# Rotating a matrix by 90 degrees: the last macro tile kept whole, with its first output stored in two halves

## The chip, the cores and the metric

One core of one Trainium2 chip. The metric is device time in microseconds (us) of a whole execution, lower is better. The profile's own span is some 1.9 us shorter than the device time of the same execution.

## The reference

```python
def setup_inputs():
    return {"x": np.random.randn(8192, 8192).astype(np.float32), "k": 1}

def reference(x, k):
    return np.rot90(x, k)
```

256 MiB are read and 256 MiB written (268.44 MB each way in the profile). There is no arithmetic; the kernel is about moving bytes.

## The kernel before

The matrix is cut into macro tiles of 1024 rows by 4096 columns. Each one is loaded as eight blocks of 128 rows (2 MB each, from the SP queue), VectorE (DVE) copies each block in eight chunks with the columns inside a group of 128 reversed, TensorE (PE) transposes 128 by 128 pieces into PSUM, ScalarE (ACT) copies PSUM to an output buffer and issues the store (2 MB each, eight per macro tile). The last macro tile is divided in two of 512 rows, and the first output of the first half is emitted ahead of the last rows' copies.

```python
R = 1024; RT = R // P
LAST = [4, 4]                    # row blocks of the last two tiles
W = 4096; CH = 512; F = 4096; FP = 2048

def macro_tiles(N, M):
    tiles = [(r0, RT, c0) for r0 in range(0, N, R) for c0 in range(0, M, W)]
    r0, _, c0 = tiles.pop()
    for n in LAST:
        tiles.append((r0, n, c0))
        r0 += n * P
    return tiles

# pools: a (row blocks) 2 buffers, ar (chunks) 63, o (outputs) 3, PSUM 2
# ... load(): per row block one DMA, then 8 DVE copies ar <- a (cut)

def store(r0, rt, c0, chunks, end):
    rows = rt * P
    PW = 1                       # column groups of one PSUM tile
    while 2 * PW * rows <= FP: PW *= 2
    G = PW                       # column groups of one output
    while 2 * G * rows <= F: G *= 2
    for i, g0 in enumerate(range(0, W // P, G)):
        if end and i % 2 == 0:   # at the end the row buffers serve outputs too
            ot = a_pool.tile([P, F], dt, tag="a")
        else:
            ot = o_pool.tile([P, F], dt, tag="o")
        # ... (cut)
        S = PW if lead or (end and r0 + rows == N and g0 + G == W // P) else G
        if i == 0 and (rt == RT or r0 + rows < N):
            # first output: transposes by row block, as the rows come
            for h in range(G // PW): psum_tile(h)
            for t in range(rt): transposes(t, range(G))
        for h in range(0, G, PW):
            # ... other outputs: transposes here (cut)
            nc.scalar.copy(o[:, G - PW - h : G - h, :], ps[h // PW])
            done = h + PW
            if done % S == 0:
                # ... dst: (g m) f -> m g f (cut)
                nc.scalar.dma_start(out=dst, in_=o[:, G - done : G - done + S, :])
        yield
```

With 1024 rows PW is 2 and G is 4, so an output has 4 groups of 1024 elements and each piece that is contiguous in DRAM is 4 KB. With 512 rows PW is 4, G is 8, and the piece is 2 KB. An output has 2 MB in both cases.

## Time and profile before

| | |
|---|---|
| device time, median of the first 3 runs | 1267.27 us (1266.35 to 1267.58) |
| span of the profiled execution | 1266.1 us |
| PE, DVE, ACT busy | 57%, 28%, 37% |
| mean transfer rate | 425 GB/s |

No compute engine is near full, and the transfers are at their rate from the second slice of the span to the 38th.

### The profile page before, as it was taken

Reading aid. Unit: us, or ns where it says so; the run is one execution under the profiler, and the core shown is the slowest. Engines: PE = TensorE matmul, PEld = TensorE weight load, DVE = VectorE, ACT = ScalarE, POOL = GpSimd, SP = SyncE. Lnnn points to the kernel's source line nnn. Section 1 sums busy time; section 2 is a strip of 40 time slices with the busy share of each in tenths; the row PEclk is TensorE's granted clock in tenths of the full one; section 3 lists DMA queues with packets and bytes.
Section 4 is the critical chain, followed back from the end, with each engine's and each line's share of the span. In section 5 each row is a group of like instructions: output and inputs, shape, how many; then the busy total and the mean of one; then the engine's idle time right before and its main releaser. Section 6 shows DMA issues by size and latency. Waiting matters only on the chain.

```text
span 1266.1 us, 10392 instructions
## 1 busy us (share of the span) xinstructions
PE 718.2 (57%) x4096; PEld 678.6 (54%) x4096; DVE 355.4 (28%) x1024; ACT 466.7 (37%) x257; POOL 0.7 (0%) x6
## 2 busy tenths in 40 slices
PE   1554565556656665556555665555655656556673
PEld 1543455555555555456554655555655655556562
DVE  4423223222232223222232223322232222322210
ACT  0432433433333333343334333343333433343363
POOL 0000000000000000000000000000000000000000
PEclk9977877777776777867778678677686686776797
DMA  9999999999999999999999999999999999999997
GB/s 399 426 428 430 428 429 427 430 429 429 429 429 429 430 428 427 430 429 430 428 430 428 429 429 428 430 428 428 430 430 428 429 429 428 428 428 428 427 399 328
DMA packets 37345, 537.55 MB, mean 425 GB/s; under 512 B 4144, under 2 KB 4144, under 8 KB 4144
## 3 DMA queue, kind: packets, MB, share of 16 engines
q10 hardware_dynamic: 18864, 268.44, 50.0%
q1 hardware_dynamic: 18432, 268.44, 49.7%
q8 instruction: 32, 0.52, 0.2%
q14 instruction: 17, 0.14, 0.0%
HBM read 268.44 MB, written 268.44 MB: 424 GB/s over the span
## 4 chain that ended last, share of the span: by engine, by line
DMA 82%; ACT 14%; PE 1%; issue 1%; ACTq 1%; DVE 0%; SPq 0%
DMA out_dram<-ot 79%; ACT ot L169 14%; DMA a<-in_x_dram 3%; PE pt L148 1%; ACTq L177 0%; DVE ar L108 0%; ACTq L169 0%; SPq L102 0%
## 5 line engine op out<-in xcount | busy, mean ns | idle before, releaser
L148 PE MATMUL pt<-ident,ar 128*128 128x128 f32 x4096 | 718.2, 356 | 528.0 <-ACT ot L169 487.6
L148 PEld LDWEIGHTS pt<-ident,ar 128*128 128x128 f32 x4096 | 678.6, 191 | 567.4 <-ACT ot L169 521.4
L169 ACT COPY ot<-pt 128x2048 f32<-128x2048 f32 x256 | 465.4, 1869 | 756.7 <-DMA out_dram<-ot 727.0
L108 DVE COPY ar<-a 128x512 f32<-128x512 f32 x1024 | 355.4, 421 | 861.1 <-DMA a<-in_x_dram 524.0
L169 ACT ACT_TABLE_LOAD x1 | 1.3, 1283 | 25.5 <-DVE ar L108 25.5
masks.py:199 POOL TENSOR_SCALAR_AFFINE_SELECT ident<-ident 128x128 f32<-128x128 f32 x1 | 0.3, 292 | 0.1
masks.py:197 POOL MEMSET ident<- 128x128 f32 x1 | 0.2, 204 | 0.3 <-POOLq L217 0.3
L217 POOL MEMSET const-bfloat16-1.0<- 128x1 bf16 x1 | 0.1, 102 | 0.0
L217 POOL MEMSET const-uint8-127<- 128x1 uint8 x1 | 0.1, 102 | 0.0
L217 POOL MEMSET const-float32-0.0<- 128x1 f32 x1 | 0.1, 99 | 0.2 <-issue 0.2
L217 POOL MEMSET const-float32-1.0<- 128x1 f32 x1 | 0.1, 99 | 0.0
## 6 DMA issues: line engine op xcount, KB each, us to landing
a<-in_x_dram SPq DMA_DIRECT2D x128, 2048.0 KB, 16.8
out_dram<-ot ACTq DMA_DIRECT2D x125, 2048.0 KB, 25.5
out_dram<-ot ACTq DMA_DIRECT2D x6, 1024.0 KB, 27.3
```

Source lines behind the costliest of these rows:

```text
L108: nc.vector.tensor_copy(out=ar[:], in_=a[:, j * CH : (j + 1) * CH].rearrange("r (b m) -> r b m", m=P)[:, :, ::-1],)
L148: nc.tensor.transpose(ps[w // PW][:, PW - 1 - w % PW, t * P : (t + 1) * P], chunks[t, g * P // CH][:, g % (CH // P), :], ident,)
L169: nc.scalar.copy(o[:, G - PW - h : G - h, :], ps[h // PW])
L217: nc = _bacc.Bacc("TRN2", target_bir_lowering=False, num_devices=1)
```

## The change

Its intent: the division into two tiles of 512 rows lets output start before the last rows are in. The change gives that up, has one simpler loop and larger contiguous rows in DRAM, and tries to keep the early start by storing the first output in two halves of 1 MB.

```diff
-LAST = [4, 4]
 def macro_tiles(N, M):
-    tiles = [...]; (last tile popped, two of 512 rows appended)
+    return [(r0, RT, c0) for r0 in range(0, N, R) for c0 in range(0, M, W)]
 ...
-            S = PW if lead or (end and r0 + rows == N and g0 + G == W // P) else G
+            S = PW if lead or (end and (i == 0 or g0 + G == W // P)) else G
 ...
-    (load and store as generators; first output of the first half emitted
-     between the last rows' load and their copies)
+    for m in tiles:
+        store(*m, load(*m), m == tiles[-1])
```

More of the change, by code (lines that the diff above doesn't have):

```diff
@@ L47, in macro_tiles @@
 def macro_tiles(N, M):
-    tiles = [(r0, RT, c0) for r0 in range(0, N, R) for c0 in range(0, M, W)]
-    r0, _, c0 = tiles.pop()
-    for n in LAST:
-        tiles.append((r0, n, c0))
-        r0 += n * P
-    return tiles
+    return [(r0, RT, c0) for r0 in range(0, N, R) for c0 in range(0, M, W)]
 @with_exitstack
@@ L104, in load @@
             )
-            yield chunks
             for j in range(W // CH):
@@ L114, in load @@
                 chunks[t, j] = ar
-            yield chunks
+        return chunks
     def store(r0, rt, c0, chunks, end):
@@ L179, in store @@
                     )
-            yield
     tiles = macro_tiles(N, M)
-    *most, before_last, last = tiles
-    for m in most:
-        *_, chunks = load(*m)
-        for _ in store(*m, chunks, False):
-            pass
-    *_, chunks = load(*before_last)
-    outputs = store(*before_last, chunks, True)
-    rows = load(*last)
-    for _ in range(2 * last[1] - 1):
-        next(rows)
-    next(outputs)
-    chunks = next(rows)
-    for _ in outputs:
-        pass
-    for _ in store(*last, chunks, True):
-        pass
+    for m in tiles:
+        store(*m, load(*m), m == tiles[-1])
 _INS = ['x', 'k']
```

## The prediction

> **What bounds the kernel now.** I read the page first: the slices, then the chain of waits. They say that the transfers fill the whole run, and which of them end it.
>
> ```profile
> DMA  9999999999999999999999999999999999999997
> GB/s 399 426 428 430 428 429 427 430 429 429 429 429 429 430 428 427 430 429 430 428 430 428 429 429 428 430 428 428 430 430 428 429 429 428 428 428 428 427 399 328
> ...
> DMA 82%; ACT 14%; PE 1%; issue 1%; ACTq 1%; DVE 0%; SPq 0%
> DMA out_dram<-ot 79%; ACT ot L169 14%; DMA a<-in_x_dram 3%; PE pt L148 1%; ACTq L177 0%; DVE ar L108 0%; ACTq L169 0%; SPq L102 0%
> ```
>
> From the second slice on the DMA engines move 426 to 430 GB/s, and only the last two slices (31.65 us each) fall, to 399 and 328. Against 428 that is (29 + 100)/428 x 31.65 = 9.5 us of transfer time missing at the end. This is all that a change to the last macro tile can touch; everything up to it is the same program. So I looked at the end in order of time, in the timeline, with the previous macro tile boundary (which is a boundary between whole tiles) for comparison:
>
> ```profile
> 1129.50 5.44 PE L148 MATMUL pt<-ident,ar 128*128 128x128 f32 x28 [4.46 <-ACT ot L169]
> ...
> 1134.98 2.77 DVE L108 COPY ar<-a 128x512 f32<-128x512 f32 x8 [7.05 <-PE pt L148]
> ...
> 1135.46 0.66 PE L148 MATMUL pt<-ident,ar 128*128 128x128 f32 x4 [0.52 <-DVE ar L108]
> ...
> 1206.29 3.63 ACT L169 COPY ot<-pt 128x2048 f32<-128x2048 f32 x2 [6.25 <-DMA out_dram<-ot]
> ...
> 1209.95 0.55 ACTq L177 DMA_DIRECT2D out_dram<-ot  x1
> ...
> 1213.59 3.64 ACT L169 COPY ot<-pt 128x2048 f32<-128x2048 f32 x2 [3.66 <-PE pt L148]
> 1213.71 2.77 DVE L108 COPY ar<-a 128x512 f32<-128x512 f32 x8 [7.10 <-DMA a<-in_x_dram]
> ...
> 1217.25 0.55 ACTq L177 DMA_DIRECT2D out_dram<-ot  x1
> ...
> 1221.56 0.55 ACTq L177 DMA_DIRECT2D out_dram<-ot  x1
> ```
>
> Counting the issues from the end, 1209.95 is the last store of the tile before; 1217.25 is the first store of the first half tile, and from there one store of 2 MB follows every 4.31 us (two ACT copies, 3.64, one issue, 0.55, small gaps). The last rows arrive at 1213.7. After that only stores are left. The first three lines show how a whole tile starts: 28 transposes of seven row blocks, and the last four 0.48 us after DVE begins on the eighth.
>
> Then the transfers in windows of 1 us (after PE, PEld, DVE, ACT and POOL come the granted clock, the DMA share and GB/s):
>
> ```profile
> 1216.00:1217.00 1.00, 1.00 (x12) 1.00 (x11) 0.49 (x2) 1.00 (x1) 0.00 (x0) 1.00 0.58 246
> 1217.00:1218.00 1.00, 1.00 (x12) 0.96 (x11) 0.00 (x0) 0.33 (x2) 0.00 (x0) 1.00 0.43 180
> 1218.00:1219.00 1.00, 1.00 (x12) 1.00 (x10) 0.00 (x0) 1.00 (x1) 0.00 (x0) 1.00 0.86 360
> ...
> 1258.00:1259.00 1.00, 0.00 (x0) 0.00 (x0) 0.00 (x0) 0.00 (x0) 0.00 (x0) 0.50 0.50 205
> 1259.00:1260.00 1.00, 0.00 (x0) 0.00 (x0) 0.00 (x0) 0.00 (x0) 0.00 (x0) 0.50 0.28 115
> 1260.00:1261.00 1.00, 0.00 (x0) 0.00 (x0) 0.00 (x0) 0.00 (x0) 0.00 (x0) 0.50 0.16 66
> ...
> 1262.00:1263.00 1.00, 0.00 (x0) 0.00 (x0) 0.00 (x0) 0.00 (x0) 0.00 (x0) 0.50 0.12 49
> 1263.00:1264.00 1.00, 0.00 (x0) 0.00 (x0) 0.00 (x0) 0.00 (x0) 0.00 (x0) 0.50 0.08 33
> ```
>
> Two separate things are missing. At 1216 to 1219 the mean share is 0.58, 0.43, 0.86, a hole of 1.1 engine-averaged us between the store of 1209.95 and that of 1217.25. But some engines keep moving in it. At the end, one engine's part of 428 GB/s is 26.8. So 205 GB/s is about eight engines, 115 four, 66 and 49 about two, 33 little more than one. Most engines finish by 1258.4; the last ones need until 1264.6, and the span ends at 1266.1. I followed the engine that ends last backwards through the packet records of the trace: from 1264.6 to before 1190 it has no pause over 0.06 us, not even at 1216 to 1219. It finishes its part of the store of 1209.95 at 1224.5, while the fast engines finish theirs at about 1216. From there it writes eight outputs at 5.02 us each: 1224.5 + 8 x 5.02 = 1264.6. This engine sets the end; the hole in the others costs nothing.
>
> **What the Trainium skill says.** "DMA: Bandwidth & Descriptors", section "Where 436 GB/s comes from", puts the ceiling at 435.2 GB/s; the trace agrees with 428 to 430 in nearly every slice. The same page, "Why a DMA increments its semaphore by 16 and not by 1", says that up to 16 engines work on a transfer and finish independently, and that only the full count means landed; "Queues, rings and completion order" says that each engine consumes its descriptors in ring order. So a late engine is not helped by an early one, which the windows show (two engines, then one, at the end). "Perfetto Trace Analysis", section "DMA Optimizations", expects larger pieces to be faster, naming "2KB → 4KB or 8KB". A row of a 512-row output is 2 KB in DRAM, of a 1024-row one 4 KB. The trace doesn't show a gain: once reads are over, the last engine takes 0.630 us per 16 KB packet in the two 4 KB-row stores before 1224.5 (10.08 us for 16) and 0.627 in the eight outputs with 2 KB rows (40.16 for 64).
>
> **The change part by part.** Loads, DVE copies (1024), transposes (4096), ACT copies (256) and bytes stay as they are. The compiled order of the instructions shows one more store, 132 instead of 131, because the first output goes out as two of 1 MB. The last output is in two halves in both.
>
> *First output.* Removed: the early start on the first half tile, whose transposes needed only its own four row blocks, so that ACT could begin at 1213.59. Now the first output needs all eight row blocks. By the boundary at 1135, the last four transposes begin 0.48 us after DVE starts at 1213.71, so at 1214.2, and end at about 1214.9; the first PSUM tile needs two of them, so ACT begins at about 1214.6. One copy is 1.82 us: the first half is issued at 1216.4 (0.8 earlier than the 1217.25 of before, but 1 MB instead of 2). Then issue 0.55, gap 0.1, copy 1.82: second half at 1218.9. Second output: + 4.31 = 1223.2 (before: 1221.56). The later ones follow at 4.31 us: the last half is issued at about 1223.2 + 6 x 4.31 + 0.65 = 1249.7, against 1250.80 before, where the last issues took 1.0 to 3.6 us each.
>
> *Fast engines.* The hole of before ended about 1.3 us after the issue. So the first MB can start at 1217.7 and lasts 2.5 us (half of 5.02), to 1220.2; the second to 1222.7; the third and fourth can't start before 1223.2 + 1.3 = 1224.5. That is a new hole of 1.8 us, after which 14 MB need 7 x 5.02 = 35.1: fast engines end at 1259.6 instead of 1258.4. They are + 1.2 worse, but 5.0 us ahead of the last one.
>
> *Last engine.* It is ready for the first output at 1224.5, 4.3 us after the second half could start; for the second at 1229.5, 5.0 after; then the margin grows by 5.02 - 4.31 = 0.7 per output. It never starves, writes the same number of packets, and ends at 1264.6 again. The additional completion costs it 0.006 us. **Sum: 0.0 us on the path that sets the end,** give or take 0.3: its packets took 0.63 to 0.645 in stretches where all engines were busy, instead of 0.626, and this may fall otherwise.
>
> **The rivals.** *(a) The hole counts.* If in the timed runs, unlike in the profiled one, no engine lags by more than the 4 to 5 us of margin, the fast engines' sum holds and the kernel loses up to 1.2 us: 1268.5. For it: I have one profile. Against it: profiled and timed runs agree (1267.99 against 1266.35 to 1267.58), and the spread comes from the steady part, which doesn't change. *(b) 4 KB rows are faster.* If the writes ran at the 0.615 us that they take while mixed with reads, 64 x 0.012 = 0.8 us would be won: 1266.5. Against it the two 4 KB-row stores above. *(c) A wait takes its place.* The fifth output waits for both halves of the first in its buffer. The last engine lands the first output at 1229.9; ACT comes to the fifth at about 1232.5, so the wait is hidden by 2.6 us. Even if it were not, ACT is done at 1249.7 and could be 10 us later. *(d) DVE's 63 buffers for 64 chunks.* The last chunk waits for a transpose of the first output, but the order of PE by row blocks frees it early, as at each whole tile before.
>
> **Range and chances.** The predicted time is that of before, 1267.3 us. Timed runs spread 1.2 us; (b) pulls 0.8 down, (a) 1.2 up, and (a) is somewhat likelier. So 1266.0 to 1268.7. Two per cent is 25 us, more than the 9.5 us that the end has to give and far more than a hole could cost: 0.99 for within 2%, the rest for an odd state of the chip.
>
> **What would show it.** In the changed profile: first issues of the last tile near 1216.4, 1218.9, 1223.2, last near 1249.7; a hole in the windows near 1222 to 1224 as well as one before 1218; a write tail whose last microseconds again show one or two engines' rate (25 to 60 GB/s), ending at 1264.6 with the span at 1266.1. It would be wrong if the tail falls from full rate to nothing within a microsecond or two (then no engine lagged, and the hole counted), if the last engine's 2 MB take 4.9 us instead of 5.02, or if ACT shows a long wait for a store after 1232.

## The result, and the profile after

The changed kernel took 1267.26 us in the median (1266.70 to 1267.84, 6 runs), the kernel before 1267.35 (1266.35 to 1267.61, 6 runs). The ratio is 1.0, with a 95% interval of 0.9987 to 1.0013. Ratios here are the mean time of one kernel's runs over that of the other's of the same rounds, so not quite the ratio of the medians.

The slices and the chain of waits of the changed kernel, as they were shown of the kernel before:

```profile
GB/s 398 428 427 432 426 428 427 430 429 430 428 430 428 429 428 429 429 430 431 427 429 429 429 428 429 430 429 427 429 430 427 423 429 430 426 428 429 429 357 377
...
DMA 82%; DVE 12%; ACT 3%; issue 1%; PE 1%; ACTq 0%; DVEq 0%; SPq 0%
DMA a<-in_x_dram 76%; DVE ar L100 12%; DMA out_dram<-ot 6%; ACT ot L161 3%; PE pt L140 1%; ACTq L169 0%; DVEq L100 0%; SPq L95 0%; ACTq L161 0%
```

The share of the DMA is the same, 82%. The chain now runs back through the loads (76%) and before through the stores (79%), though the program and the rates are the same up to the last tile: where loads and stores fill the same engines, which of the two the chain names says little. The last two slices are 357 and 377 instead of 399 and 328: the shortfall has moved from the last slice to the one before, and its sum is hardly changed ((71 + 51)/428 x 31.65 = 9.0 us against 9.5). The timeline of the changed kernel (start, duration, engine, line, operation, count, idle time before and what ended it) says why:

```profile
1208.19 5.90 PE L140 MATMUL pt<-ident,ar 128*128 128x128 f32 x28 [3.72 <-ACT ot L161]
...
1215.30 2.77 DVE L100 COPY ar<-a 128x512 f32<-128x512 f32 x8 [7.95 <-DMA a<-in_x_dram]
...
1215.78 0.66 PE L140 MATMUL pt<-ident,ar 128*128 128x128 f32 x4 [1.68 <-DVE ar L100]
1216.25 3.64 ACT L161 COPY ot<-pt 128x2048 f32<-128x2048 f32 x2 [6.35 <-PE pt L140]
1218.15 2.32 ACTq L169 DMA_DIRECT2D out_dram<-ot  x2
...
1218.17 8.18 PE L140 MATMUL pt<-ident,ar 128*128 128x128 f32 x48 [1.74 <-ACT ot L161]
...
1226.54 0.55 ACTq L169 DMA_DIRECT2D out_dram<-ot  x1
```

The first output waits for all eight row blocks, as foreseen: 28 transposes early, the last four 0.48 us after DVE starts. But DVE starts at 1215.30, 1.6 us later than before, and the second output is stored at 1226.54, not at 1223.2, since the 48 transposes from 1218.17 on (its own 32 and the next output's first 16) took 8.18 us. That is 170 ns each, against 3.74/32 = 117 ns in the kernel before. The windows of 1 us (the clock that was granted, DMA share and GB/s are the last three columns) show the clock and the new hole:

```profile
1218.00:1219.00 1.00, 0.83 (x4) 0.83 (x5) 0.07 (x1) 1.00 (x2) 0.00 (x0) 0.50 0.35 147
...
1221.00:1222.00 1.00, 1.00 (x6) 1.00 (x6) 0.00 (x0) 0.11 (x1) 0.00 (x0) 0.50 1.02 418
...
1225.00:1226.00 1.00, 1.00 (x12) 1.00 (x11) 0.00 (x0) 1.00 (x1) 0.00 (x0) 1.00 0.18 66
1226.00:1227.00 1.00, 0.79 (x8) 0.55 (x7) 0.00 (x0) 0.51 (x1) 0.00 (x0) 1.00 0.12 49
...
1261.00:1262.00 1.00, 0.00 (x0) 0.00 (x0) 0.00 (x0) 0.00 (x0) 0.00 (x0) 0.50 0.98 410
...
1263.00:1264.00 1.00, 0.00 (x0) 0.00 (x0) 0.00 (x0) 0.00 (x0) 0.00 (x0) 0.50 0.19 82
1264.00:1265.00 1.00, 0.00 (x0) 0.00 (x0) 0.00 (x0) 0.00 (x0) 0.00 (x0) 0.50 0.04 16
```

While the clock stood at 0.50, PE made some six transposes per us. At 1225 to 1227 only 66 and 49 GB/s move, which is two engines at 26.8; the others stand still, most of them for some 3.3 us in the packet records. Then full rate holds until about 1262.5, four microseconds longer than before, and three engines finish alone. The end is where it was.

The trace records a completion of every store by each of the 16 DMA engines. For the last store of all, the middle one of the sixteen comes at 1258.9 before and at 1262.8 after, but the last one at 1265.0 and 1264.9. (Behind the others come two engines before, at 1264.0 and 1265.0, and three after, at 1264.7 to 1264.9.) So most engines got nearly 4 us later and the time did not move.

### The profile page after: what moved, and what is told of

Read it like the earlier page. It is cut to its first block, busy times and chain, and to the rows that moved or that the text cites. A ratio compares the mean times of both kernels' runs of the same rounds, so it can differ in the third digit from the quotient of the medians.

```text
span 1266.0 us, 10392 instructions
## 1 busy us (share of the span) xinstructions
PE 727.8 (57%) x4096; PEld 686.1 (54%) x4096; DVE 355.3 (28%) x1024; ACT 466.7 (37%) x257; POOL 0.7 (0%) x6
## 4 chain that ended last, share of the span: by engine, by line
DMA 82%; DVE 12%; ACT 3%; issue 1%; PE 1%; ACTq 0%; DVEq 0%; SPq 0%
DMA a<-in_x_dram 76%; DVE ar L100 12%; DMA out_dram<-ot 6%; ACT ot L161 3%; PE pt L140 1%; ACTq L169 0%; DVEq L100 0%; SPq L95 0%; ACTq L161 0%
## 5 line engine op out<-in xcount | busy, mean ns | idle before, releaser
L140 PE MATMUL pt<-ident,ar 128*128 128x128 f32 x4096 | 727.8, 359 | 522.3 <-ACT ot L161 461.4
L140 PEld LDWEIGHTS pt<-ident,ar 128*128 128x128 f32 x4096 | 686.1, 192 | 563.8 <-ACT ot L161 496.2
```

The costliest lines, as they stand in the source:

```text
L140: nc.tensor.transpose(ps[w // PW][:, PW - 1 - w % PW, t * P : (t + 1) * P], chunks[t, g * P // CH][:, g % (CH // P), :], ident,)
```

## The experiments

Two theories. **L**: the DMA engine that ends last sets the end; the others may stand idle so long as they don't pass it. **H**: the hole is paid, the end follows the point at which the stores are fed. For all eleven runs (names with b_ start from the kernel before, with a_ from the changed one) the results are correct. The first two columns are issue times of the last tile's first store and of its second output, the next two completions of the last store:

| kernel | first store | 2nd output | middle engine | last engine | median time | ratio to before (95%) |
|---|---|---|---|---|---|---|
| before | 1217.25 | 1221.56 | 1258.9 | 1265.0 | 1267.35 | |
| changed | 1218.15 | 1226.54 | 1262.8 | 1264.9 | 1267.26 | 1.0 (0.9987 to 1.0013) |
| a_warm | 1216.95 | 1223.03 | 1259.3 | 1264.4 | 1267.32 | 0.9996 (0.9984 to 1.0009) |
| a_onestore | 1219.11 | 1223.41 | 1260.3 | 1264.3 | 1266.98 | 0.9997 (0.9985 to 1.001) |
| b_firsthalves | 1215.84 | 1221.92 | 1258.8 | 1264.8 | 1267.87 | 1.0004 (0.9991 to 1.0017) |
| b_late2 | 1220.73 | 1225.54 | 1262.3 | 1264.5 | 1267.46 | 1.0002 (0.999 to 1.0015) |
| a_late2 | 1218.43 | 1226.51 | 1262.8 | 1264.7 | 1267.56 | 1.0002 (0.999 to 1.0015) |
| a_rowlate | 1224.09 | 1231.72 | 1268.0 | 1269.9 | 1270.87 | 1.0027 (1.0015 to 1.004) |
| b_late5 | 1226.66 | 1228.4 | 1268.6 | 1270.1 | 1273.34 | 1.005 (1.0037 to 1.0062) |
| a_late5 | 1218.56 | 1229.63 | 1268.4 | 1270.3 | 1272.88 | 1.0046 (1.0032 to 1.006) |

The profiles are one execution each, so read their last decimals with care; a_rowlate's was the slowest of its five. The runs were made in three groups on three chips, each beside the kernel before, which had medians of 1267.20 to 1267.51.

### Delays before the first store: b_late2, a_late2, b_late5, a_late5

```diff
-                nc.scalar.copy(o[...], ps[h // PW])
+                for _ in range(3 if <end, first output, h == 0> else 1):   # 6 in *_late5
+                    nc.scalar.copy(o[...], ps[h // PW])
```

> The kernel before, with the first ACT copy of the first half tile's first output done three times instead of once: the first store and all after it come 2 x 1.83 = 3.7 us later, nothing else changes. Theory L (the last DMA engine sets the end, the hole in the others is free): most engines end at 1258.3 + 3.7 = 1262.0, still before the last one at 1264.6, which gets its work in time (first store can start by 1222.2, it needs it at 1224.5), so the time changes by 0.0 us (within 0.5). Rival H (every microsecond in which the stores come late is paid): + 3.7 us, a ratio of 1.0029.

Measured: ratio 1.0002. The delay did happen: the first store went out 3.5 us later and the second 4.0 us later, and the hole became deep. Here are windows of b_late2:

```profile
1219.00:1220.00 1.00, 1.00 (x6) 1.00 (x6) 0.00 (x0) 1.00 (x1) 0.00 (x0) 0.50 0.12 49
1220.00:1221.00 1.00, 1.00 (x6) 0.60 (x5) 0.00 (x0) 0.90 (x2) 0.00 (x0) 0.50 0.12 49
...
1262.00:1263.00 1.00, 0.00 (x0) 0.00 (x0) 0.00 (x0) 0.00 (x0) 0.00 (x0) 0.50 0.24 98
1263.00:1264.00 1.00, 0.00 (x0) 0.00 (x0) 0.00 (x0) 0.00 (x0) 0.00 (x0) 0.50 0.16 66
```

At 1219 to 1221 two engines move, the rest wait. Most engines end at 1262.3 instead of 1258.9, the last at 1264.5. H's 1.0029 lies outside the interval. A delay of 3.5 us was free, as L said.

> The changed kernel with the same delay of 3.7 us before its first half store. Here most engines end at 1262.8 in the profile and the last one at 1264.5, so only 1.7 us are free. Theory L: most engines become the bound, 1262.8 + 3.7 = 1266.5, that is + 1.9 to 2.0 us (ratio 1.0015 to 1.0016). Rival H: + 3.7 us, as for the kernel before.

Measured: ratio 1.0002, so neither value. The run did not do what I meant. The compiled order put the repeated copies among the next ones: the second half store came 2.3 us later, but the second output at 1226.51, where it was without the delay (1226.54), and that one fixes the point from which the stores run without a break. There was almost no delay where it counts, and the run tells nothing about a delay.

> The kernel before with a delay of 5 x 1.83 = 9.15 us. Theory L: the last engine now starves too, from 1224.5 to 1217.25 + 9.15 + 1.3 = 1227.7, 3.2 us, and most engines end at 1258.3 + 9.15 = 1267.5; so + 3 us (2.5 to 3.7). Rival H: + 9.2 us.

Measured: ratio 1.0050, some 6 us; L said 3, H 9.2. The first store was 9.4 us late. With its 1.3 us of start and eight outputs of 5.02 us most engines would end at 1268.1, and they did at 1268.6. What L missed is that the last engine, which had been stopped by the starvation, was 1.5 us behind the rest again at the end (1270.1). So a late engine's lag is not only brought along, it also forms anew. The packet records show where. The page lists a queue of packets of the kind "instruction" (here of the kernel before):

```profile
q8 instruction: 32, 0.52, 0.2%
```

These packets have 16 KB each, and one comes about every 39 us. In b_late5 one ran from 1228.32 to 1229.20, just as the starved engines started, and the packet after it took 1.02 us. One engine's part of the first output then landed at 1235.00, those of the fifteen others at 1233.26 to 1233.48. A second one came at 1251.52, and from the next store on two engines were late.

> The changed kernel with a delay of 9.15 us. Theory L: most engines end at 1262.8 + 9.15 = 1272.0, so 9.15 less the free 1.7 = + 7.4 us (7 to 8), some 4 us more than the same delay costs the kernel before. Rival H: + 9.2 us for both.

Measured: ratio 1.0046, less than both. As in a_late2 the order moved, and further: the second output (2 MB) was issued at 1229.63, 3.1 us late and not 9.15, and ahead of the first output's second half, which followed at 1231.39. Between the first half and that point the engines ran dry:

```profile
1226.00:1227.00 1.00, 0.18 (x2) 0.00 (x0) 0.00 (x0) 1.00 (x1) 0.00 (x0) 1.00 0.00 0
...
1230.00:1231.00 1.00, 1.00 (x7) 1.00 (x6) 0.00 (x0) 1.00 (x1) 0.00 (x0) 0.50 0.66 262
```

From 1229.63 with 1.3 us of start and the remaining 15 MB (7.5 times 5.02 us) most engines would end at 1268.6, and the middle one did at 1268.4.

### The same delay earlier: a_rowlate

To be rid of the reordering, the delay was put ahead of the transposes, on DVE:

```diff
-                nc.vector.tensor_copy(out=ar[:], in_=...)
+                for _ in range(10 if <last row block, j == 0> else 1):
+                    nc.vector.tensor_copy(out=ar[:], in_=...)
```

> The changed kernel with the DVE copy of the first chunk of the last rows repeated, so that both halves of the first output and the second output come some 15 x 0.346 = 5.2 us later (in the run with repeated ACT copies the instruction order moved so that the second output was not late). Theory L: most engines end at 1262.8 + 5.2 = 1268.0 and pass the last engine, which starves 1231.7 + 1.3 - 1230.1 = 2.9 us and ends at 1267.4: + 3.5 us. Rival H: + 5.2 us. A delay that is free: 0.

Measured: 1270.87 against 1267.46 in the median, + 3.4 us, ratio 1.0027. The second output was 5.2 us late, just as planned. L's 3.5 us fits; H's 5.2 us would be 1.0041, just outside the interval. That the delay was free in part is what the medians say; the fit to 0.1 us is partly luck. In the profiled execution (1272.79, the slowest) most engines ended at 1268.0, as L said, but the end came at 1269.9, where L had 1267.4. There the starvation had brought all sixteen engines into step, and one fell 1.9 us behind later: around an instruction packet at 1252.21 (0.95 us) three write packets took 0.89 to 1.00 us instead of 0.61, and at the next store one engine landed at 1255.25 and the others at 1253.06 to 1253.47. L had no term for that, and the other four executions were 1.8 to 2.9 us shorter.

### The hole taken away: a_warm

```diff
                 for t in range(rt):
+                    if end and t == rt - 1:
+                        for u in (4, 5, 6):      # done a second time
+                            transposes(u, range(G))
                     transposes(t, range(G))
```

> The changed kernel with 12 of the first output's transposes done twice, so that PE does not stand idle while the last rows arrive (it waited 1.7 us there and then ran the second output's 48 transposes at a granted clock of 0.5, 8.2 us). If the idle time is what lowers the clock, the second output's store is issued at about 1223 to 1224 instead of 1226.5 and the hole of the fast engines shrinks by 2 to 3 us. Theory L (last engine sets the end): the time stays, 0.0 within 0.5 us, as the last engine never starved. Rival H (the hole counts): - 2 to - 3 us. If the clock stays at 0.5 all the same, nothing moves and the run only says that these transposes are not enough.

Timeline and windows of a_warm:

```profile
1216.95 2.31 ACTq L172 DMA_DIRECT2D out_dram<-ot  x2
1216.97 3.73 PE L140 MATMUL pt<-ident,ar 128*128 128x128 f32 x32 [1.74 <-ACT ot L164]
...
1223.03 0.55 ACTq L172 DMA_DIRECT2D out_dram<-ot  x1
```

```profile
1221.00:1222.00 1.00, 0.72 (x7) 0.72 (x8) 0.00 (x0) 1.00 (x2) 0.00 (x0) 1.00 1.09 459
...
1259.00:1260.00 1.00, 0.00 (x0) 0.00 (x0) 0.00 (x0) 0.00 (x0) 0.00 (x0) 0.50 0.22 90
...
1262.00:1263.00 1.00, 0.00 (x0) 0.00 (x0) 0.00 (x0) 0.00 (x0) 0.00 (x0) 0.50 0.12 49
```

At 1221 PE works at a clock of 1.00, the second output goes out at 1223.03, 3.5 us earlier, and the long hole is gone. Most engines end 3.5 us earlier, at 1259.3. The time stays: 0.9996. The tail from 1259 to 1264 is again one of few engines. H needs at least - 2 us (0.9984), which is the edge of the interval. Whether the additional transposes raised the clock isn't shown: in a_onestore, which doesn't have them, PE also had 1.00 at this point and the second output came at 1223.41.

### Each part of the change alone: a_onestore, b_firsthalves

```diff
 a_onestore:
-            S = PW if lead or (end and (i == 0 or g0 + G == W // P)) else G
+            S = PW if lead or (end and g0 + G == W // P) else G
 b_firsthalves:
-            S = PW if lead or (end and r0 + rows == N and g0 + G == W // P) else G
+            S = PW if lead or (end and r0 + rows < N and i == 0) or (end and r0 + rows == N and g0 + G == W // P) else G
```

> The changed kernel with its first output stored in one piece, so only the first part of the change (whole tile) is left. The first store comes at about 1219.9 instead of 1218.15, the second output's as before at 1226.5, so most engines end where they did, the last engine is still fed in time (it needs the first output at about 1225). Theory L: 0.0 within 0.5 us. Rival H: the first hole grows by 1.8 us and the second shrinks by as much, so + 0 to + 1.8 us.

Measured: 0.9997. The whole tile alone costs nothing that the interval can show. The first hole was longer (down to 49 GB/s at 1219), the second gone.

> The kernel before with the first output of its first half tile stored in two halves, so only the second part of the change. The first half is issued about 1.8 us earlier than 1217.25 and fills most of the hole of 1.1 engine-averaged us; most engines end 1 to 2 us earlier. Theory L: 0.0 within 0.5 us. Rival H: - 1 to - 2 us.

Measured: 1.0004. The halves alone filled most of the first hole (1.03 of the DMA engines' time at 1217 to 1218, where the kernel before had 0.43), but the middle engine ended only 0.1 us earlier, less than I expected, since the second output's issue was as before. The end did not move. Both parts are worth 0.0 within about 1.7 us, so the result is not two larger effects that cancel.

### A last store without half of the engines: b_half8

```diff
+                    if <last half store>:
+                        for p in range(0, P, 8):
+                            nc.sync.dma_start(out=dst[p : p + 8], in_=o[p : p + 8, ...])
```

> The kernel before with its last half store (1 MB) cut into 16 stores of 8 partitions, which can use at most 8 of the 16 DMA engines, always the same ones. Engines left out have 2.5 us less to do, the 8 used have 2.5 us more. Theory L: if both late engines are among those left out, the end comes at 1264.6 - 2.5 = 1262.1, so - 2.5 us; if one or both are among those used, + 2.5 us, 1267.1. Rival H (the sum of bytes over all engines sets the end, the late engines are only an effect of the order): + 2.5 us for 8 engines that do double work, minus what they had to spare; it has no way to - 2.5.

Measured: 1.0062, + 7.9 us in the median, which neither theory said. The timeline of b_half8 tells what I had left out:

```profile
1248.19 21.93 SPq L179 DMA_DIRECT2D out_dram<-ot  x16
```

SP needed 21.9 us for the 16 stores: 14.9 us in the issues themselves (0.65 to 2.08 us each), and most of the rest in two waits, until the last engine had completed an earlier store (at 1261.20 and 1263.82; the next issues came at 1261.22 and 1263.84). The last bytes landed at 1272. The issue set the end, so the run does not answer its question. Each of these stores did use eight engines: it left 8 data packets and 8 completion packets, and the mean share of the DMA engines stayed at 0.44 to 0.55 from 1265 to 1270. The run does hint that it could not have helped: while these stores ran, the two late engines took 6.1 us for an output instead of 5.0, so they seem to be among the eight that were used.

### The size of the rows: a_rows512, a_rows256

```diff
-R = 1024
+R = 512      # a_rows256: 256
```

> The changed kernel with R = 512 throughout: every store writes rows of 2 KB instead of 4 KB, same bytes and stores of 2 MB. Alone, the last engine's 16 KB packets took 0.626 us with 2 KB rows and 0.616 with 4 KB rows. If the row size costs this in mixed traffic too: 128 stores x 8 packets per engine x 0.010 = + 10 us, ratio 1.008. If it costs only when writes run alone: the 8 last stores lose 8 x 8 x 0.010 = + 0.6 us, and the time stays within 1 us of the others, apart from what the smaller tiles do to the start and the end.

Measured: 1279.23 us, ratio 1.0091 (1.0078 to 1.0105). The rate in the slices of a_rows512 is lower all along, mostly 425 or 426 instead of 428 to 430:

```profile
GB/s 392 412 425 420 411 426 424 426 425 426 425 425 426 426 426 426 425 426 425 426 426 424 426 426 424 425 423 426 426 426 422 424 426 426 425 425 425 425 400 339
```

In the packet records between 100 and 1100 us a write of 16 KB takes 0.626 us in the mean, against 0.616 in the changed kernel, and a read 0.614 against 0.612. An engine handles 1024 of each: 1024 x (0.0099 + 0.0019) = 12.1 us, which is the difference. So rows of 2 KB cost, with reads beside them too.

> The changed kernel with R = 256: rows of 1 KB in DRAM, again stores of 2 MB. With 4 KB rows the write packets of the middle took 0.615 us in the median, with 2 KB rows 0.624, and the kernel with 2 KB rows throughout was 11.7 us slower. If the cost goes by the number of rows in a packet (4, 8, 16), a packet takes about 0.642 and the kernel is 128 x 8 x 0.027 = 28 us slower than with 4 KB rows, some 1295; if it is a single step below 4 KB, it stays at about 1279.

Measured: 1411.88 us, ratio 1.1157, far above both values. The write packet is 0.640 us in the median, as foreseen, but the stores can no longer be issued fast enough. From the chain of waits of a_rows256, and from the query for the line that issues (count, shortest, median and longest issue in ns):

```profile
ACTq L169 48%; ACT ot L161 27%; DMA a<-in_x_dram 17%; DVE ar L100 2%; DMA out_dram<-ot 2%; PE pt L140 1%; ACTq L161 0%; DVEq L100 0%; SPq L95 0%
```

```profile
L169 ACTq DMA_DIRECT2D out_dram<-ot x130: 546/6672/11177, 19.0 to 1394.1; - x130
```

One issue takes 6.7 us instead of 0.55 and keeps ACT from its copies. Half of the chain is now the issue itself. That is another limit than the packet's length.

## Why the prediction was right

**What sets the end** was right, and it is shown, not only argued. Over seven kernels, one profile each (before, changed, a_warm, a_onestore, b_firsthalves, b_late2, a_late2) the middle engine ends anywhere from 1258.8 to 1262.8, the last one from 1264.3 to 1265.0, and the ratios are 0.9996 to 1.0004. Where the middle engine passes 1265 (a_rowlate, the two late5) the time rises.

**The first output.** Predicted issues 1216.4, 1218.9 and, for the second output, 1223.2; measured 1218.15, 1219.9, 1226.54. Three terms were mis-sized. The last rows came at 1215.30 instead of 1213.71; in the trace one of their packets, on the last engine, took 1.21 us instead of 0.61, and the load 17.6 us. Each of the ten profiles has one such packet (1.21 or 1.22 us, between 1207 and 1210), so what differs is the engine that it falls on. In a_warm DVE started on the last rows at 1213.27, so this is scatter between executions. I added the issue's 0.55 us between the two copies of an output that is stored in halves, but the second copy ran straight on, so the halves are 1.77 us apart and not 2.5. And the second output's transposes ran at a clock of 0.50. Where the clock was 1.00 (a_warm), the second output came at 1223.03, within 0.2 us of the predicted time.

**Most engines** were to end at 1259.6. In the changed kernel it was 1262.8, for these reasons, and in a_warm 1259.3. So the margin of 5.0 us was only 1.9 in the profiled execution; it was enough. The prediction's "fast engines", done with the store of 1209.95 at about 1216, were only the first six; in the completion records (0.3 to 0.4 us after the packets) these come at 1216.45 to 1216.60, and the middle engine at 1218.1.

**The last engine** was to end at 1264.6, and its last packet came at 1264.46. But the term in it was wrong: it takes 4.91 us per output, not 5.02. The prediction had named 4.9 us as a sign that it would be wrong, and this sign came. That the end still fell on 1264.6 is luck: two misses of 0.7 and 0.9 us cancelled. Its packets took 0.616 us with rows of 4 KB, constantly from 1215 on. My reading, that the trace shows no gain from 4 KB rows, failed: I compared with two stores whose packets took 0.615 to 0.655 us on that engine, and a_rows512 shows what rows of 2 KB cost. Why those packets of before were slower I have not settled. So rival (b) was half right. In that execution it won 0.9 us (39.3 us from 1225.2 instead of 40.2 from 1224.5), and the engine had started on the last tile 0.7 us later. The completion of the store before it, by the last engine, ranges from 1224.2 to 1225.9 over the ten profiles of the table, so the 0.7 is scatter too. From that completion to the end the last engine took 40.1, 40.1 and 40.3 us in before, b_firsthalves and b_late2 (2 KB rows), and 39.3, 39.8, 39.7 and 40.4 in the changed kernel, a_warm, a_onestore and a_late2 (4 KB rows), so the gain does not come every time. A true gain of up to 0.8 us may be left; the interval of 1.7 us either way can't show it.

**Rivals (c) and (d)** did not appear: no copy of ACT waited for a store in the last tile of the changed kernel.

What stays open: why two engines run behind the others (4 to 6 us behind the middle one where no hole lets them catch up), and which they are. Part of an answer is in b_late5, a_late5 and a_rowlate: where a starvation had brought the engines into step, one or two became late again, by 1.0 to 1.9 us each, where an instruction packet had run. Whether such packets also make the 4 to 6 us was not traced.

## What to carry to other kernels

In a transfer-bound kernel look at who ends last among the 16 DMA engines before working on holes in their mean: in the last microseconds of the windows the rate falls in steps of a sixteenth, and an engine that is still behind makes every hole of the others free up to its lag. A test costs little: delay the feed by as much as you hope to win; if the time stays, so will it when you win it. And where the writes are half of the traffic, as here, prefer rows of 4 KB in DRAM to shorter ones (longer ones were not tried).

## What the Trainium skill lacked or had wrong

- "DMA: Bandwidth & Descriptors", "Specifications", gives 512 B as the least transfer for line rate. With stores of 2 MB from 128 partitions, rows of 2 KB in DRAM took 0.626 us per 16 KB where rows of 4 KB took 0.616 (1.6%; the kernel 0.9% slower), and with rows of 1 KB an issue from ACT took 6.7 us in the median instead of 0.55 (the kernel 11.6% slower). The page gives no time of an issue by the number of rows on this chip.
- The same page, "Latency and other measured facts", tells of two engines that are usually slower and guesses at the rings of the GpSimd path. This kernel issues from SP and ACT only, and two engines still end several microseconds after the middle one wherever the feed is not delayed (5.0 and 6.1 us in the kernel before, 4.1 and 5.1 in a_warm), and its profile has no queue of that path, so the guess doesn't fit here. In b_late5 and a_rowlate a new lag of 1.5 and 1.9 us formed where an instruction packet of 16 KB ran. The page has no word on what such a lag does to holes.
- "Perfetto Trace Analysis", "DMA Optimizations", says that splitting transfers may let a task end sooner if the DMA engines are generally idle. Over this run they are not (nine tenths or more in every slice but the last), but in the hole the mean share was down to 0.43. Here the split filled a hole of most engines (share 1.03 instead of 0.43 in its deepest window), and the ratio was 1.0004: a mean share of the engines doesn't tell if the last one is idle.
